# Up-projection blocks of a gated MLP: both 12-bit parts of the tokens in one 512-column product

## The chip, the cores and the metric

The kernel runs on one core of one Trainium2 chip. The metric is the device time of one execution in microseconds. The engines are TensorE (PE; its weight loads, which overlap the products, are listed as PEld), VectorE (DVE), ScalarE (ACT), GpSimd (POOL) and SyncE (SP, which here issues the DMAs).

## The reference, cut to what matters

Two decoder layers over 256 tokens of width 1024, in float32. A layer has a mixer (retention, attention and short convolution), an output projection with layer norm, and a gated MLP with layer norm. The change is in the MLP:

```
def conv_ffn(h, w_up, ffn_conv_w, w_down):
    u = h @ w_up
    a, b = u[..., :D_FF], u[..., D_FF:]
    a = causal_dwconv(a, ffn_conv_w)
    return (jax.nn.gelu(a.astype(F32), approximate=False) * b.astype(F32)).astype(h.dtype) @ w_down
```

D_FF is 2816, that is 22 feature tiles of 128; the contraction over D_MODEL = 1024 has 8 K tiles of 128; causal_dwconv has three taps.

## The kernel before, in words

Every float32 operand of the large products is held as two parts in the type float32r, a high part and the remainder (`split`, L80 to L82: an ACT copy makes the high part, a DVE subtraction the low one). A product of two such operands is three products: high by high, low by high, and high by low.

The weights come as units of 128 rows by 1024 columns in the order of the list `units` (L86 to L110). `prepare` (L120) loads a unit by DMA into one of five `raw` buffers and splits it into `whi` (L81, ACT) and `wlo` (L82, DVE), of which there are SLOTS = 6 each. `weights` (L143) asks for the units up to LOOKAHEAD = 5 beyond the one that is wanted now. So the cast of a unit waits until PE is done with the unit that had its buffer before.

The tokens, transposed, are the tiles `xh` and `xl` (128 partitions, 8 K tiles, 256 tokens). They are written at the start by `load_first` (L151) and afterwards by `turn` (L561), which transposes 128 tokens on PE and splits the result; both are allocated anew for each half of a layer (L555, L665).

In the MLP of a layer, feature tiles 0 and 1 are computed ahead with the tokens as the stationary operand (`first_up`, L584), tile 2 by halves (L626). Then a loop over f (L650) computes the up projection of tile f+1 (`up`, L621: two calls of `feature_block`, L297, one for a and one for b), takes the down-projection weights of tile f, and adds tile f's part to four PSUM banks (L658 to L660: `out_mm`, which calls `mm3`, L229, four times, so 12 products of 512 columns). The last tiles' down products are held back and done after the loop. A `feature_block` is 8 K tiles of three products of 256 columns (L302 to L304), summed in the left half of a PSUM bank (`acc`, four banks). `gated` (L606) turns a and b into h: z = a times tap 2 (L608, ACT), two more taps (L609 and L611, DVE), Gelu (L613, ACT), times b (L615, DVE), and the split into `hh` (L81, ACT) and `hl` (L82, DVE), which are the stationary operands of the down products.

The program is traced in this order; a planner of the framework then fixes the order in each engine's queue by its own estimate of times, and puts in the waits.

Of the kernel before, what the change touches and what calls it, by code (L numbers as in the profile page):

```python
# [11 lines left out]
F32R = mybir.dt.float32r  # L12
# [4 lines left out]
P = 128  # L17
D = 1024
T = 256
# [7 lines left out]
KD = D // P  # L27
# [17 lines left out]
FILL = (2, 1, 1, 2)  # L45
AT = ((7, 8), (7, 8), (6, 8), (20, 22))
WARM = 6
HALVES = (slice(0, HD), slice(HD, P))


@with_exitstack
def hybrid_decoder(ctx: ExitStack, tc: tile.TileContext, x, xT, wv, wf, wt, w_out, wg, w_up, w_down,
                   conv_w, ffn_w, ln1_g, ln1_b, ln2_g, ln2_b, rel_bias,
                   c_ident, c_rot, c_decay, c_bucket, out):
    nc = tc.nc
    cp = ctx.enter_context(tc.tile_pool(name="cp", bufs=1))
    wp = ctx.enter_context(tc.tile_pool(name="wp", bufs=1))
    xp = ctx.enter_context(tc.tile_pool(name="xp", bufs=1))
# [6 lines left out]
    def acc():  # L65
        return pa.tile([P, 512], F32, name="acc", tag="acc")

    def att():
        return pb.tile([P, 512], F32, name="att", tag="att")

    def big(dtype, name):
        return wp.tile([P, 1024], dtype, name=name, tag="big", bufs=2 * TAIL)
# [7 lines left out]
    def split(dst_hi, dst_lo, src):  # L80
        nc.scalar.copy(dst_hi, src)  # L81
        nc.vector.tensor_sub(dst_lo, src, dst_hi.bitcast(F32))  # L82
# [37 lines left out]
    def prepare(upto):  # L120
        while state["next"] < min(upto, len(units)):
            key, src, held = units[state["next"]]
            r = raw()
            if held:
                hi, lo = big(F32R, "hhi"), big(F32R, "hlo")
            else:
                hi = wp.tile([P, 1024], F32R, name="whi", tag="whi", bufs=SLOTS)
                lo = wp.tile([P, 1024], F32R, name="wlo", tag="wlo", bufs=SLOTS)
            if len(src.shape) == 2:
                nc.sync.dma_start(r, src)  # L130
                convert(key, hi, lo, r, 1024)
            elif state["next"] < KD:
                load_first(state["next"], r, src, hi, lo)
            else:
                k, c = src.shape[1:]
                nc.sync.dma_start(r[:, :k * c].rearrange("p (k c) -> p k c", k=k), src)
                convert(key, hi, lo, r, k * c)
            ready[key] = (hi, lo)
            state["next"] += 1
            if state["next"] >= 7 and spread:  # L140
                spread.pop(0)()

    def weights(*key, ahead=LOOKAHEAD):  # L143
        prepare(index[key] + 1 + ahead)
        return ready.pop(key)


    xh = xp.tile([P, KD, T], F32R, name="xh", tag="xh")
    xl = xp.tile([P, KD, T], F32R, name="xl", tag="xl")

    def load_first(k, r, src, hi, lo):  # L151

# [19 lines left out]
    def warm_up():  # L172
# [3 lines left out]
        ps = att()  # L176
        for i in range(WARM):
            nc.tensor.matmul(ps[:, :P], zero, zero, start=True, stop=True)
# [80 lines left out]
    def fetch_table(func, after):  # L259

        nc.scalar.activation(sp.tile([P, 1], F32, name="table", tag="table", bufs=1), after[:, :1], func)
# [11 lines left out]
    for k in range(KD):  # L273
        hi, lo = weights(0, "v", k)
        for g in range(NV):
            c = slice(g * VG, g * VG + VG)
# [7 lines left out]
    for l in range(DEPTH):  # L284
# [12 lines left out]
        def feature_block(*name):  # L297
            hi, lo = weights(l, *name)
            ps = acc()
            for k in range(KD):  # L300
                c = slice(k * P, k * P + P)
                nc.tensor.matmul(ps[:, :T], hi[:, c], xh[:, k, :], start=k == 0, stop=False)  # L302
                nc.tensor.matmul(ps[:, :T], hi[:, c], xl[:, k, :], start=False, stop=False)  # L303
                nc.tensor.matmul(ps[:, :T], lo[:, c], xh[:, k, :], start=False, stop=k == KD - 1)  # L304
            return ps
# [6 lines left out]
        class Pair:  # L312
# [9 lines left out]
            def scores(self, ps, c128, c256):  # L322

                for lhs, rhs, c, first, last in (
# [3 lines left out]
                        (self.narrow_hi, self.wide_lo, c256, False, True)):  # L328
                    for r, p in zip(HALVES, ps):
                        nc.tensor.matmul(p[:, c], lhs[r], rhs[r], start=first, stop=last)  # L330

        def buf256(name):
            return ap.tile([P, T], F32, name=name, tag="b256", bufs=3)

        moba = [Pair() for _ in range(3)]
        for i, m in enumerate(moba):
            p = feature_block(f"mq{i}")[:, :T]
# [4 lines left out]
        for i, m in enumerate(moba):  # L342
            p = feature_block(f"mk{i}")[:, :T]
# [113 lines left out]
        def moba_values(j):  # L457

            po = att()
            for t, s in ((0, slice(0, T)), (1, slice(T, 3 * P))):  # L460
                for h, r in zip((2 * j, 2 * j + 1), HALVES):
                    nc.tensor.matmul(po[r, t * P:T], mv[t][:, h * HD:h * HD + HD], prob[h][:, s],
# [60 lines left out]
        for t, p in enumerate(token_group("rg")):  # L523
            c, g = slice(t * HW, t * HW + HW), slice(t * NH, t * NH + NH)
            y, gt = yn[:, c], gate[:, c]
# [11 lines left out]
        ps = [[acc() for _ in range(2)] for _ in range(NT)]  # L537
# [5 lines left out]
        def late_mm(t):  # L543
            return [lambda h=h, n=n: out_mm(t, h, *late[n], False, n == len(late) - 1)
                    for h in range(2) for n in range(len(late))]

        for n, k in enumerate(WO_ORDER[:-TAIL]):
            hi, lo = weights(l, "wo", k)
# [3 lines left out]
        late = [weights(l, "wo", k) + (ch[:, k, :], cl[:, k, :]) for k in WO_ORDER[-TAIL:]]  # L552
        gw = [weights(l, "g", i, ahead=SLOTS - 1 - i) for i in range(4)]
        x1 = xp.tile([P, NT, D], F32, name="x1", tag="xtok", bufs=2)
        xh = xp.tile([P, KD, T], F32R, name="xh", tag="xh")  # L555
        xl = xp.tile([P, KD, T], F32R, name="xl", tag="xl")

        def norm(t, xin, g, b, xout):
            layer_norm(t, ps[t], xin, g, b, xout)
# [4 lines left out]
        def weave(steps, t, xout, at):  # L564

            for i, step in enumerate(steps):
                for h in range(2):
                    if at[h] == i:
                        turn(t, xout, h)
                step()  # L570
            for h in range(2):
                if at[h] >= len(steps):
                    turn(t, xout, h)
# [32 lines left out]
        def gated(f, a, b):  # L606
            z = sp.tile([P, T], F32, name="za", tag="f256", bufs=6)
            nc.scalar.mul(z, a, fw[:, l, f, 2:3])  # L608
            nc.vector.scalar_tensor_tensor(z[:, 1:], a[:, :T - 1], fw[:, l, f, 1:2], z[:, 1:],  # L609
                                           op0=ALU.mult, op1=ALU.add)  # L610
            nc.vector.scalar_tensor_tensor(z[:, 2:], a[:, :T - 2], fw[:, l, f, 0:1], z[:, 2:],  # L611
                                           op0=ALU.mult, op1=ALU.add)
            nc.scalar.activation(z, z, AF.Gelu)  # L613
            hf = sp.tile([P, T], F32, name="hf", tag="f256", bufs=6)
            nc.vector.tensor_mul(hf, z, b)  # L615
            hh = sp.tile([P, T], F32R, name="hh", tag="hh", bufs=LAST + 1)
            hl = sp.tile([P, T], F32R, name="hl", tag="hl", bufs=LAST + 1)
            split(hh, hl, hf)
            return hh, hl

        def up(f):  # L621
            a = feature_block("up", f, 0)[:, :T]
            return gated(f, a, feature_block("up", f, 1)[:, :T])

        a = []
# [6 lines left out]
        ps = [[att() for _ in range(2)] for _ in range(NT)]  # L632

        def value_group(vt, vw, g, t):

            bank = []

            def step(k):
                if k == 0:
                    bank.append(acc())  # L640
                hi, lo = vw[g][k // 4]
                c = slice(k % 4 * VG, k % 4 * VG + VG)
                mm3(bank[0][:, :VG], xh[:, k, tokens(t)], xl[:, k, tokens(t)], hi[:, c], lo[:, c],
                    k == 0, k == KD - 1)
                if k == KD - 1:
                    nc.scalar.copy(vt[t][:, g * VG:g * VG + VG], bank[0][:, :VG])
            return [lambda k=k: step(k) for k in range(KD)]
# [14 lines left out]
        if l + 1 < DEPTH:  # L662
            fetch_table(AF.Exp, late[-1][2].bitcast(F32))
            vw = [[weights(l + 1, "v", g, i, ahead=SLOTS - 1 - 2 * g - i) for i in range(2)] for g in range(NV)]
            xh = xp.tile([P, KD, T], F32R, name="xh", tag="xh")  # L665
            xl = xp.tile([P, KD, T], F32R, name="xl", tag="xl")
            for step in late_mm(0):
                step()
            norm(0, x1, g2, b2, x2)
            weave(late_mm(1), 0, x2, AT[1])  # L670
            norm(1, x1, g2, b2, x2)
            vt = [big(F32, "v") for _ in range(NT)]
            for t in range(NT):
                steps = []
                for g in range(NV):
                    steps += value_group(vt, vw, g, t)
                if t == 0:
                    weave(steps, 1, x2, AT[3])
                else:
                    for step in steps:  # L680
                        step()
        else:
            for t in range(NT):
                for step in late_mm(t):
                    step()
                layer_norm(t, ps[t], x1, g2, b2, x2, lambda s: nc.sync.dma_start(out[tokens(t), s], x2[:, t, s]))
# [72 lines left out]
```

## Time and profile before

| | us |
|---|---|
| median of 3 runs | 631.47 (631.27 to 631.86) |
| the profiled execution, its own time | 632.78 |
| span of the profiled execution | 631.0 |
| PE busy | 617.9 |
| DVE busy | 436.1 |
| ACT busy | 332.3 |

The span runs from the first to the last instruction of the profiled execution; its own time has some 1.8 us around it. A matmul's record overlaps the next one's, so its duration (283 ns for 256 columns) isn't what it costs; the distance between starts is. The granted TensorE clock is given as a share of full speed, 0.996 over the span. L302 is line 302 of the kernel before.

### The profile page before, as it was taken

What the parts mean: (1) busy time and instruction counts of PE and PEld (TensorE: products, weight loads), DVE (VectorE), ACT (ScalarE), POOL (GpSimd) and SP (SyncE); (2) the same over time, 40 slices, a digit from 0 to 9 for tenths busy, and PEclk for the clock granted to TensorE, in tenths of its full rate; (3) what the DMA queues carried; (4) which work ended last, traced back from release to release, by engine and by line L of the source; (5) the groups of instructions that cost most, each with busy time, mean ns of one, the idle gap of its engine ahead of it and who ended that gap; (6) DMA issues with size and microseconds to landing.
All of it is one profiled execution on the core that took longest, in us unless ns stands there. A gap on an engine that the chain in (4) does not pass through costs nothing.

```text
span 631.0 us, 11073 instructions
## 1 busy us (share of the span) xinstructions
PE 617.9 (98%) x4350; PEld 574.1 (91%) x4350; DVE 436.1 (69%) x774; ACT 332.3 (53%) x581; POOL 14.1 (2%) x14
## 2 busy tenths in 40 slices
PE   8999999999999999999999999999999999999994
PEld 7898899879999999999899999987999999999993
DVE  4468789877566565677766687888865665657746
ACT  4569936245544545466336795371745445455620
POOL 0000002000000000000000000101000000000001
PEclk9999999999999999999999999999999999999998
DMA  6996545745655555567427435572656565556401
GB/s 209 282 380 231 163 158 182 263 131 197 202 176 196 175 193 177 190 227 273 135 68 265 139 106 161 159 254 117 220 184 193 178 194 176 196 181 195 159 1 66
DMA packets 37163, 115.99 MB, mean 184 GB/s; under 512 B 4049, under 2 KB 9464, under 8 KB 37112
## 3 DMA queue, kind: packets, MB, share of 16 engines
q1 hardware_dynamic: 37112, 115.30, 55.3%
q8 instruction: 34, 0.56, 0.4%
q14 instruction: 17, 0.14, 0.1%
HBM read 114.22 MB, written 1.06 MB: 183 GB/s over the span
## 4 chain that ended last, share of the span: by engine, by line
PE 86%; DMA 5%; DVE 4%; ACT 1%; SPq 1%; issue 1%; POOL 0%; DVEq 0%; ACTq 0%; POOLq 0%
PE acc L304 13%; PE acc L303 13%; PE acc L302 13%; PE att L230 6%; PE att L231 6%; PE att L232 6%; PE acc L231 5%; PE acc L232 5%; PE acc L230 5%; PE acc L391 4%; PE acc L392 4%; PE acc L393 4%; DMA raw<-in_wf_dram 3%; DMA raw<-in_wv_dram 2%; PE att L330 1%
## 5 line engine op out<-in xcount | busy, mean ns | idle before, releaser
L82 DVE TENSOR_TENSOR wlo<-raw,whi 128x1024 fp32r<-128x1024 f32 (+3 forms) x207 | 229.5, 1115 | 138.2 <-ACT whi L81 137.6
L81 ACT CAST whi<-raw 128x1024 fp32r<-128x1024 f32 (+3 forms) x207 | 197.6, 962 | 197.1 <-PE acc L303 102.9
L304 PE MATMUL acc<-xh,wlo 128*128 128x256 f32 x720 | 203.7, 283 | 0.0
L303 PE MATMUL acc<-xl,whi 128*128 128x256 f32 x720 | 203.7, 283 | 0.0
L302 PE MATMUL acc<-xh,whi 128*128 128x256 f32 x720 | 203.6, 283 | 0.0
L302 PEld LDWEIGHTS acc<-xh,whi 128*128 128x128 f32 x720 | 138.1, 192 | 1.4
L303 PEld LDWEIGHTS acc<-xl,whi 128*128 128x128 f32 x720 | 138.1, 192 | 1.3
L304 PEld LDWEIGHTS acc<-xh,wlo 128*128 128x128 f32 x720 | 138.1, 192 | 0.2
L391 PE MATMUL acc<-xh,whi 128*128 128x256 f32 x208 | 61.3, 295 | 0.0
L392 PE MATMUL acc<-xl,whi 128*128 128x256 f32 x208 | 58.8, 283 | 0.0
L393 PE MATMUL acc<-xh,wlo 128*128 128x256 f32 x208 | 58.8, 283 | 0.0
L231 PE MATMUL att<-whi,hl 128*128 128x512 f32 x144 | 56.5, 392 | 0.0
L232 PE MATMUL att<-wlo,hh 128*128 128x512 f32 x144 | 56.0, 389 | 0.0
L230 PE MATMUL att<-whi,hh 128*128 128x512 f32 x144 | 55.7, 394 | 0.0
L230 PE MATMUL acc<-whi,xh 128*128 128x256 f32 (+2 forms) x144 | 47.1, 331 | 1.2 <-ACT whi L81 1.2
L231 PE MATMUL acc<-whi,xl 128*128 128x256 f32 (+2 forms) x144 | 46.3, 324 | 0.8 <-DVE xl L82 0.8
L232 PE MATMUL acc<-wlo,xh 128*128 128x256 f32 (+2 forms) x144 | 45.8, 323 | 0.1
L391 PEld LDWEIGHTS acc<-xh,whi 128*128 128x128 f32 x208 | 39.6, 190 | 2.6 <-issue 1.0
L392 PEld LDWEIGHTS acc<-xl,whi 128*128 128x128 f32 x208 | 39.6, 191 | 0.2
L393 PEld LDWEIGHTS acc<-xh,wlo 128*128 128x128 f32 x208 | 39.6, 191 | 0.1
L232 PEld LDWEIGHTS att<-wlo,hh 128*128 128x128 f32 x144 | 27.1, 188 | 5.8
L230 PEld LDWEIGHTS att<-whi,hh 128*128 128x128 f32 x144 | 27.0, 189 | 4.8
(136 smaller groups left out, 805.3 us busy)
## 6 DMA issues: line engine op xcount, KB each, us to landing
raw<-in_w_up_dram SPq DMA_DIRECT2D x80, 512.0 KB, 3.7
raw<-in_w_down_dram SPq DMA_DIRECT2D x44, 512.0 KB, 3.7
raw<-in_wf_dram SPq DMA_DIRECT2D x36, 512.0 KB, 4.4
raw<-in_w_out_dram SPq DMA_DIRECT2D x16, 512.0 KB, 4.2
raw<-in_wg_dram SPq DMA_DIRECT2D x8, 512.0 KB, 4.3
raw<-in_wt_dram SPq DMA_DIRECT2D x8, 384.0 KB, 3.1
raw<-in_wv_dram SPq DMA_DIRECT2D x6, 512.0 KB, 4.8
raw<-in_wv_dram SPq DMA_DIRECT2D x7, 384.0 KB, 5.6
```

Source lines behind the costliest of these rows:

```text
L81: nc.scalar.copy(dst_hi, src)
L82: nc.vector.tensor_sub(dst_lo, src, dst_hi.bitcast(F32))
L230: nc.tensor.matmul(ps, lhi, rhi, start=first, stop=False)
L231: nc.tensor.matmul(ps, llo, rhi, start=False, stop=False)
L232: nc.tensor.matmul(ps, lhi, rlo, start=False, stop=last)
L302: nc.tensor.matmul(ps[:, :T], hi[:, c], xh[:, k, :], start=k == 0, stop=False)
L303: nc.tensor.matmul(ps[:, :T], hi[:, c], xl[:, k, :], start=False, stop=False)
L304: nc.tensor.matmul(ps[:, :T], lo[:, c], xh[:, k, :], start=False, stop=k == KD - 1)
L330: nc.tensor.matmul(p[:, c], lhs[r], rhs[r], start=first, stop=last)
L391: nc.tensor.matmul(ps[:, :T], hi[:, c], xh[:, k, :], start=k == 0, stop=False)
L392: nc.tensor.matmul(ps[:, :T], hi[:, c], xl[:, k, :], start=False, stop=False)
L393: nc.tensor.matmul(ps[:, :T], lo[:, c], xh[:, k, :], start=False, stop=k == KD - 1)
```

## The change

The tiles `xh` and `xl` become the two halves of one tile `xx` (128 partitions, 8 K tiles, 2 parts, 256 tokens). For feature tiles 3 to 17 of both layers, `up` calls `wide_block`: per K tile one product of the high weight part with both token parts (512 columns, a whole PSUM bank) and one of the low weight part with the high token part (256 columns, added to the right half). Then an ACT copy takes the right half out of PSUM into a tile `feat` (three buffers, of a tag that the mixer uses too), and a DVE addition adds the left half to it. `gated` reads a and b from these tiles in place of PSUM. Feature tiles 0 to 2 and 18 to 21 stay as they were.

```diff
+WIDE = range(3, 18)
...
-    xh = xp.tile([P, KD, T], F32R, name="xh", tag="xh")
-    xl = xp.tile([P, KD, T], F32R, name="xl", tag="xl")
+    def parts():
+
+        x = xp.tile([P, KD, 2, T], F32R, name="xx", tag="xx")
+        return x, x[:, :, 0, :], x[:, :, 1, :]
+
+    xx, xh, xl = parts()
...
+        def wide_block(*name):
+
+
+            hi, lo = weights(l, *name)
+            ps = acc()
+            for k in range(KD):
+                c = slice(k * P, k * P + P)
+                nc.tensor.matmul(ps, hi[:, c], xx[:, k].rearrange("p s t -> p (s t)"), start=k == 0, stop=False)
+                nc.tensor.matmul(ps[:, T:], lo[:, c], xx[:, k, 0, :], start=False, stop=k == KD - 1)
+            y = buf256("feat")
+            nc.scalar.copy(y, ps[:, T:])
+            nc.vector.tensor_add(y, ps[:, :T], y)
+            return y
+
         def up(f):
+            if f in WIDE:
+                a = wide_block("up", f, 0)
+                return gated(f, a, wide_block("up", f, 1))
             a = feature_block("up", f, 0)[:, :T]
             return gated(f, a, feature_block("up", f, 1)[:, :T])
```

The two later allocations of `xh` and `xl` (L555, L665) become calls of `parts` in the same way.

## Rows read from the trace of the kernel before

**Rows 1.** The page: span, busy times, and the chain that ended last by engine.
```profile
span 631.0 us, 11073 instructions
...
PE 617.9 (98%) x4350; PEld 574.1 (91%) x4350; DVE 436.1 (69%) x774; ACT 332.3 (53%) x581; POOL 14.1 (2%) x14
...
PE 86%; DMA 5%; DVE 4%; ACT 1%; SPq 1%; issue 1%; POOL 0%; DVEq 0%; ACTq 0%; POOLq 0%
```

**Rows 2.** Windows: one loop turn, layer 0; the loop's stretch of layer 1.
```profile
core 0: us, PE busy (x) PEld busy (x) DVE busy (x) ACT busy (x) POOL busy (x), PEclk, DMA share, GB/s
157.00:165.50 8.50, 8.50 (x63) 8.01 (x62) 5.21 (x9) 4.14 (x6) 0.00 (x0) 1.00 0.68 227
464.00:583.00 119.00, 119.00 (x843) 112.13 (x842) 74.18 (x100) 58.95 (x85) 0.00 (x0) 1.00 0.58 189
```

**Rows 3.** Waits, 464 to 583 us, the whole answer: total us, times, longest.
```profile
DVE wlo L82 <- ACT whi L81: 44.3, 42, 1.4
ACT whi L81 <- PE acc L303: 42.2, 28, 1.6
ACT whi L81 <- PE att L231: 17.8, 14, 1.3
```

**Rows 4.** Groups by line and shape: busy us, mean ns, idle before.
```profile
L302 PE MATMUL acc<-xh,whi 128*128 128x256 f32 x720 | 203.6, 283 | 0.0
```

**Rows 5.** Timeline of PE, one loop turn of layer 0: start us, duration us.
```profile
200.07 0.40 PE L230 MATMUL att<-whi,hh 128*128 128x512 f32 x1
200.31 0.40 PE L231 MATMUL att<-whi,hl 128*128 128x512 f32 x1
200.54 0.39 PE L232 MATMUL att<-wlo,hh 128*128 128x512 f32 x1
...
202.59 0.39 PE L232 MATMUL att<-wlo,hh 128*128 128x512 f32 x1
202.82 0.28 PE L302 MATMUL acc<-xh,whi 128*128 128x256 f32 x1
202.93 0.28 PE L303 MATMUL acc<-xl,whi 128*128 128x256 f32 x1
...
208.57 0.40 PE L230 MATMUL att<-whi,hh 128*128 128x512 f32 x1
```

**Rows 6.** Timeline of PE, output projection of layer 0: first and last of 39 starts.
```profile
105.95 0.39 PE L232 MATMUL acc<-wlo,cath 128*128 128x512 f32 x1
...
114.79 0.39 PE L232 MATMUL acc<-wlo,cath 128*128 128x512 f32 x1
```

**Rows 7.** Groups by line and shape: a PSUM copy and a DVE operation on PSUM.
```profile
L615 DVE TENSOR_TENSOR hf<-za,acc 128x256 f32<-128x256 f32 x44 | 18.2, 413 | 2.5 <-PE acc L304 1.4 <-ACT za L613 1.1
...
L646 ACT COPY v<-acc 128x256 f32<-128x256 f32 x6 | 2.2, 370 | 5.5 <-PE acc L232 5.4
```

**Rows 8.** Timeline of all engines, layer 0, gating chain of one feature tile.
```profile
155.73 0.47 ACT L608 ACTIVATE za<-acc,fw 128x256 f32<-128x256 f32 x1
...
157.65 1.05 ACT L81 CAST whi<-raw 128x1024 fp32r<-128x1024 f32 x1 [1.46 <-PE acc L303]
...
160.29 1.05 ACT L81 CAST whi<-raw 128x1024 fp32r<-128x1024 f32 x1 [1.27 <-PE att L231]
...
162.52 0.42 DVE L82 TENSOR_TENSOR hl<-hf,hh 128x256 fp32r<-128x256 f32 x1
...
163.27 1.05 ACT L81 CAST whi<-raw 128x1024 fp32r<-128x1024 f32 x1 [1.63 <-PE acc L303]
...
166.07 0.40 PE L230 MATMUL att<-whi,hh 128*128 128x512 f32 x1
```

**Rows 9.** Timeline of all engines, layer 1 value projection with the last turn.
```profile
326.21 0.36 PE L230 MATMUL acc<-whi,xh 128*128 128x256 f32 x1
...
326.50 0.59 ACT L81 CAST xh<-att 128x512 fp32r<-128x512 f32 x1 [0.57 <-PE att L268]
```

**Rows 10.** Timeline of PE, loop start of layer 0.
```profile
150.09 0.28 PE L303 MATMUL acc<-xl,whi 128*128 128x256 f32 x1
150.27 1.19 PE L230 MATMUL att<-whi,hh 128*128 128x512 f32 x4
151.30 0.28 PE L304 MATMUL acc<-xh,wlo 128*128 128x256 f32 x1
```

More of the change, by code (lines that the diff above doesn't have):

```diff
@@ L554, in hybrid_decoder @@
         x1 = xp.tile([P, NT, D], F32, name="x1", tag="xtok", bufs=2)
-        xh = xp.tile([P, KD, T], F32R, name="xh", tag="xh")
-        xl = xp.tile([P, KD, T], F32R, name="xl", tag="xl")
+        xx, xh, xl = parts()
         def norm(t, xin, g, b, xout):
@@ L664, in hybrid_decoder @@
             vw = [[weights(l + 1, "v", g, i, ahead=SLOTS - 1 - 2 * g - i) for i in range(2)] for g in range(NV)]
-            xh = xp.tile([P, KD, T], F32R, name="xh", tag="xh")
-            xl = xp.tile([P, KD, T], F32R, name="xl", tag="xl")
+            xx, xh, xl = parts()
             for step in late_mm(0):
```

## The prediction, made before the change was run

> **What bounds the kernel now.** I read the page first. TensorE (PE) is busy 617.9 of 631.0 us, and the chain that ended last runs 86% over PE [rows 1]. A busy PE proves little by itself, since matmul records overlap, so I went on to the stage that the change touches: the loop over feature tiles f, once per layer. In its windows PE is busy all the time, at the full granted clock (1.00), while DVE has 5.21 and ACT 4.14 of 8.50 us and DMA stands at 0.58 to 0.68 [rows 2]. Then the waits of that stage: ACT's weight casts wait for PE to free a weight buffer, and DVE waits for ACT [rows 3]. PE is in no row of that answer, which has these three rows in all for 119 us. So PE sets the pace there, and what counts is the distance from one product's start to the next, not the 283 ns of a record [rows 4].
>
> The timeline of PE gives that distance [rows 5]. From 202.82 to 208.57 us stand two up blocks, 48 products of 256 columns: 5.75 us / 48 = 119.8 ns each. Ahead of them, from 200.07 to 202.82, stand the 12 products of 512 columns of one down-projection step. One turn of the loop is 8.50 us. In a long run of 512-column products, 39 starts from 105.95 to 114.79, the distance is 8.84 / 39 = 226.7 ns [rows 6]. So 256 more columns cost 226.7 - 119.8 = 106.9 ns, which is 2.4 columns per ns, and 119.8 - 106.9 = 12.9 ns come with each product and its weight load, whatever its width. **That 12.9 ns is what the change can take away**; the columns stay.
>
> **The change part by part.** Per K tile the three products (256 columns each) become one of 512 (high weight part times both token parts) and one of 256 (low part times high tokens), with two weight loads for three.
>
> Before, a K tile takes 3 x 119.8 = 359.4 ns. After, if each product keeps the price of its own long run, 226.7 + 119.8 = 346.5 ns: 12.9 ns less. There are 15 feature tiles x 2 blocks x 2 layers x 8 K tiles = 480 such K tiles: 480 x 12.9 ns = **6.2 us less on PE**. It lies wholly on the path, since PE waits for nothing there.
>
> No stretch before alternates the two widths, so I bound the price by the starts next to a change of width [rows 5]. Dear end: the first two 512-column products behind 256-column ones take 200.07 to 200.54, 235 ns each; 3 x 119.8 - 235 - 119.8 = 4.6 ns, x 480 = 2.2 us less. Cheap end: the first 256-column product behind 512-column ones takes 202.82 to 202.93, 110 ns; 359.4 - 226.7 - 110 = 22.7 ns, x 480 = 10.9 us less. Both are transients of one or a few products, and the long runs lie between them, so I take 12.9 ns and keep both ends.
>
> Added per block, 60 in all: an ACT copy of 128x256 out of PSUM (370 ns, by the copy of L646) and a DVE add of the same size (413 ns, by L615, which also reads a PSUM operand) [rows 7]. That makes 0.74 us of ACT and 0.83 us of DVE per turn: ACT 4.14 + 0.74 = 4.88, DVE 5.21 + 0.83 = 6.04, in a turn of 8.50 - 16 x 0.0129 = 8.29 us. Neither fills it. I cost them at nothing; PE's products hide them. Without that cover they would be 60 x 0.78 = 47 us.
>
> What waits behind them: on ACT the next weight cast stands behind the copy. That cast fills a buffer that PE needs some five units later (LOOKAHEAD = 5, a block of 2.88 us each), so 0.4 us doesn't reach PE. The path that has a deadline is the gating chain of the tile itself (L608 to the split of hf). In the turn shown, z starts at 155.73, the last step hl starts at 162.52 and takes 0.42, so it ends at 162.94, and the first product that reads hl follows the one at 166.07 by 0.23 us [rows 8]: slack 166.30 - 162.94 = 3.36 us. A copy and an add ahead of it make it 0.78 us later, and the turn is 0.21 us shorter: 2.4 us of slack remain. Cost nothing. The PSUM banks (four, two per turn) come free at the add, no later than before.
>
> The DMA issues stay as many and as large; a turn shorter by 2.4% lifts a DMA share of 0.58 to some 0.60 [rows 2], and nothing in that stage waits for a transfer [rows 3]. Nothing.
>
> The merged token tile (xh and xl as halves of one tile) changes no instruction's size. It could only cost if reads of one half were made to wait for writes of the other. The trace shows such tracking to be by element rather than by range: the product at 326.21 reads xh of the first 128 tokens and starts before the ACT cast at 326.50, queued earlier in the program, writes the same K tiles' other 128 tokens in between [rows 9]. Nothing, in load_first and in the turns alike.
>
> **Sum.** The profiled execution took 632.78 us (span 631.0): 632.78 - 6.2 = 626.6. The median of the runs is 1.3 us lower, 631.47, so **625.3 us**; the ends are 631.47 - 10.9 = 620.6 and 631.47 - 2.2 = 629.3.
>
> **The rivals.** (1) The 12.9 ns doesn't leave with the product. In an alternating stream every 512-column product could be paid as the one at 200.07 to 200.31 is, 0.24 us, as much as the two products that it replaces [rows 5]: saved 0, 631.5 us, no change. For it: every 512-column product would now stand right behind a 256-column one. Against: within the same down step the distance falls back to the long run's. Chance 0.07. [...]
>
> (2) Slower: the gating chain comes late. ACT and DVE work their queues in a fixed order, and casts that wait for PE stand in them at 157.65, 160.29 and 163.27 [rows 8]. If the later z, gelu or hh falls behind one cast more, the chain loses up to 163.27 - 160.29 = 2.98 us beside its own 0.78: 3.76 against 3.36 - 0.21 = 3.15, so PE waits 0.6 us in each of 30 turns: 631.47 - 6.2 + 18 = 643 us. It decides from the point where the chain loses a whole cast's turn; one queue place among short operations isn't enough. Against it: the order in the queues is planned and not the program's own, as the four down products at 150.27 in the midst of an up block show [rows 10], so a late chain can be planned around. Chance 0.09.
>
> (3) The wide product could be split in the build into two of 256 columns: 631.5 us, no change. The 512-column rows of the down step are single records [rows 5], so 0.02.
>
> **How the numbers follow.** Forecast 0.82, rivals 0.07, 0.09 and 0.02. About 0.2% (1.26 us) is what a measurement of this kernel can tell from no change. The forecast with both ends lies beyond that on the fast side: faster 0.82. No change: (1) and (3), 0.09. Slower: (2), 0.09. The range is the forecast's own, 620.6 to 629.3; it leaves the rivals out, 0.18 together.
>
> **What would show it.** Right: L302 to L304 keep 720 - 480 = 240 records each; the wide block's two lines have 480 each; a turn of the loop takes near 8.29 us; PE waits for nothing in the stage; ACT and DVE gain 60 operations each, some 22 and 25 us. In the PE timeline a 512- and a 256-column start together span 347 ns. Wrong: a pair at 355 to 360 ns (rival 1); PE or its weight loads waiting for hh or hl (rival 2); twice the wide records (rival 3); a stage outside the loop that changes by over a microsecond.

## The result and the profile after

The changed kernel takes 628.57 us (median of five runs, 628.15 to 629.26), the kernel before 631.86 us beside it (631.27 to 632.47): a ratio of 0.9946, 95% interval 0.9935 to 0.9958. It is faster, by 3.3 us where 6.2 were forecast. The profiled execution is the slowest of the five, 629.26 us; its page, to be read beside [rows 1], has the span, the busy times, and the chain by engine:

```profile
span 627.5 us, 10205 instructions
...
PE 614.0 (98%) x3870; PEld 547.3 (87%) x3870; DVE 456.5 (73%) x834; ACT 352.0 (56%) x641; POOL 14.1 (2%) x14
...
PE 88%; DVE 5%; DMA 3%; ACT 1%; issue 1%; SPq 1%; POOL 0%; DVEq 0%; ACTq 0%; POOLq 0%
```

PE has 4350 - 3870 = 480 products and 480 weight loads less, as counted. DVE gained 20.4 us and ACT 19.7 us for the 60 adds and 60 copies; their records below are 25.1 and 21.5 us, and overlap their neighbours in part. Line numbers have moved by some: the down products of L230 to L232 are now L235 to L237, the wide product is L632, the narrow one L633, the copy L635, the add L636. In the groups by line and shape (busy us, mean ns, idle before):

```profile
L632 PE MATMUL acc<-xx,whi 128*128 128x512 f32 x480 | 170.8, 398 | 0.0
...
L633 PE MATMUL acc<-xx,wlo 128*128 128x256 f32 x480 | 134.9, 281 | 0.0
...
L636 DVE TENSOR_TENSOR feat<-acc,feat 128x256 f32<-128x256 f32 x60 | 25.1, 418 | 0.0
L635 ACT COPY feat<-acc 128x256 f32<-128x256 f32 x60 | 21.5, 358 | 0.0
```

The waits of the loop's stretch in layer 1, 464 to 580 us, which answer to [rows 3], have these five rows and no more:

```profile
DVE wlo L83 <- ACT whi L82: 25.7, 28, 1.4
ACT whi L82 <- PE acc L632: 20.9, 14, 1.6
ACT za L612 <- DVE feat L636: 19.0, 14, 1.4
DVE za L613 <- ACT za L612: 7.5, 13, 0.6
ACT whi L82 <- PE att L236: 7.3, 14, 0.5
```

PE still waits for nothing there. The new step shows as a wait of ACT for DVE (z waits for the sum of the two halves), which costs nothing, since no wait of PE follows from it. So the missing 3 us are not in a wait. They are in the distances on PE. The timeline of PE in the changed kernel, with the two up blocks of one turn (16 pairs) from 200.57 to 206.21, and the starts of the down step of two turns, 13 turns apart:

```profile
164.28 0.40 PE L235 MATMUL att<-whi,hh 128*128 128x512 f32 x1
...
200.57 0.39 PE L632 MATMUL acc<-xx,whi 128*128 128x512 f32 x1
200.80 0.28 PE L633 MATMUL acc<-xx,wlo 128*128 128x256 f32 x1
200.91 0.40 PE L632 MATMUL acc<-xx,whi 128*128 128x512 f32 x1
201.14 0.28 PE L633 MATMUL acc<-xx,wlo 128*128 128x256 f32 x1
201.26 0.40 PE L632 MATMUL acc<-xx,whi 128*128 128x512 f32 x1
201.50 0.28 PE L633 MATMUL acc<-xx,wlo 128*128 128x256 f32 x1
201.62 0.40 PE L632 MATMUL acc<-xx,whi 128*128 128x512 f32 x1
...
206.21 0.40 PE L235 MATMUL att<-whi,hh 128*128 128x512 f32 x1
...
273.31 0.40 PE L235 MATMUL att<-whi,hh 128*128 128x512 f32 x1
```

A pair takes 5.64 us / 16 = 352.5 ns, not 346.5. The first pair behind the down products takes 200.57 to 200.91, 0.34 us; the next ones 0.35 and 0.36: the wide product stays as dear as the first ones behind narrow products were in the kernel before [rows 5]. A turn is 109.03 us / 13 = 8.387 us against 110.50 / 13 = 8.500 before (166.07 in [rows 8] to 276.57): 0.113 us less where 0.206 were forecast.

```profile
276.57 0.40 PE L230 MATMUL att<-whi,hh 128*128 128x512 f32 x1
```

Thirty turns make 3.4 us, about the measured difference.

### The profile page after: what moved, and what is told of

It is laid out like the page before. It is cut to its first block, busy times and chain, and to the rows that moved or that the text cites. A ratio compares the mean times of both kernels' runs of the same rounds, so it can differ in the third digit from the quotient of the medians.

```text
span 627.5 us, 10205 instructions
## 1 busy us (share of the span) xinstructions
PE 614.0 (98%) x3870; PEld 547.3 (87%) x3870; DVE 456.5 (73%) x834; ACT 352.0 (56%) x641; POOL 14.1 (2%) x14
## 4 chain that ended last, share of the span: by engine, by line
PE 88%; DVE 5%; DMA 3%; ACT 1%; issue 1%; SPq 1%; POOL 0%; DVEq 0%; ACTq 0%; POOLq 0%
PE acc L632 18%; PE acc L633 9%; PE att L235 6%; PE att L236 6%; PE att L237 6%; PE acc L308 5%; PE acc L309 5%; PE acc L307 5%; PE acc L396 4%; PE acc L236 4%; PE acc L237 4%; PE acc L235 4%; PE acc L397 4%; PE acc L398 4%; PE att L335 1%; DMA raw<-in_w_up_dram 1%
## 5 line engine op out<-in xcount | busy, mean ns | idle before, releaser
L632 PE MATMUL acc<-xx,whi 128*128 128x512 f32 x480 | 170.8, 398 | 0.0
L633 PE MATMUL acc<-xx,wlo 128*128 128x256 f32 x480 | 134.9, 281 | 0.0
L632 PEld LDWEIGHTS acc<-xx,whi 128*128 128x128 f32 x480 | 90.2, 188 | 21.9
L633 PEld LDWEIGHTS acc<-xx,wlo 128*128 128x128 f32 x480 | 90.8, 189 | 1.3
L308 PE MATMUL acc<-xx,whi 128*128 128x256 f32 x240 | 68.0, 283 | 0.0
L309 PE MATMUL acc<-xx,wlo 128*128 128x256 f32 x240 | 68.0, 283 | 0.0
L307 PE MATMUL acc<-xx,whi 128*128 128x256 f32 x240 | 68.0, 283 | 0.0
L396 PE MATMUL acc<-xx,whi 128*128 128x256 f32 x208 | 61.4, 295 | 0.0
L397 PE MATMUL acc<-xx,whi 128*128 128x256 f32 x208 | 58.9, 283 | 0.0
L398 PE MATMUL acc<-xx,wlo 128*128 128x256 f32 x208 | 58.8, 283 | 0.0
L237 PE MATMUL att<-wlo,hh 128*128 128x512 f32 x144 | 56.1, 390 | 0.0
L235 PE MATMUL att<-whi,hh 128*128 128x512 f32 x144 | 55.7, 394 | 0.0
L235 PE MATMUL acc<-whi,xx 128*128 128x256 f32 (+2 forms) x144 | 46.9, 330 | 1.6 <-ACT whi L82 1.6
L236 PE MATMUL acc<-whi,xx 128*128 128x256 f32 (+2 forms) x144 | 46.1, 323 | 0.8 <-DVE xx L83 0.8
L307 PEld LDWEIGHTS acc<-xx,whi 128*128 128x128 f32 x240 | 46.1, 192 | 0.1
L308 PEld LDWEIGHTS acc<-xx,whi 128*128 128x128 f32 x240 | 46.1, 192 | 0.1
L309 PEld LDWEIGHTS acc<-xx,wlo 128*128 128x128 f32 x240 | 46.1, 192 | 0.0
L237 PE MATMUL acc<-wlo,xx 128*128 128x256 f32 (+2 forms) x144 | 45.6, 321 | 0.1
L396 PEld LDWEIGHTS acc<-xx,whi 128*128 128x128 f32 x208 | 39.6, 190 | 2.6 <-issue 1.0
```

Of the source, the lines that this page charges most:

```text
L235: nc.tensor.matmul(ps, lhi, rhi, start=first, stop=False)
L236: nc.tensor.matmul(ps, llo, rhi, start=False, stop=False)
L237: nc.tensor.matmul(ps, lhi, rlo, start=False, stop=last)
L632: nc.tensor.matmul(ps, hi[:, c], xx[:, k].rearrange("p s t -> p (s t)"), start=k == 0, stop=False)
L633: nc.tensor.matmul(ps[:, T:], lo[:, c], xx[:, k, 0, :], start=False, stop=k == KD - 1)
```

## The experiments

In each of them the edit is against the changed kernel. Theories: A, a change of the product's width costs time on PE by itself; B, a narrow product is dear because it adds to PSUM columns just written; C, the added copy and add take PE's time; D, a narrow product is too short to cover the next weight load.

**Grouped: all wide products of a block, then all narrow ones.**

```diff
-            for k in range(KD):
-                c = slice(k * P, k * P + P)
-                nc.tensor.matmul(ps, hi[:, c], xx[:, k].rearrange("p s t -> p (s t)"), start=k == 0, stop=False)
-                nc.tensor.matmul(ps[:, T:], lo[:, c], xx[:, k, 0, :], start=False, stop=k == KD - 1)
+            for k0 in range(0, KD, 8):
+                for k in range(k0, k0 + 8):
+                    c = slice(k * P, k * P + P)
+                    nc.tensor.matmul(ps, hi[:, c], xx[:, k].rearrange("p s t -> p (s t)"), start=k == 0, stop=False)
+                for k in range(k0, k0 + 8):
+                    c = slice(k * P, k * P + P)
+                    nc.tensor.matmul(ps[:, T:], lo[:, c], xx[:, k, 0, :], start=False, stop=k == KD - 1)
```

> The changed kernel has a mean of 352.5 ns for a 512- and a 256-column product together, where the long runs of each width give 226.7 + 119.8 = 346.5 ns. Here a block does its 8 wide products first and its 8 narrow ones after them: one change of width each way per block in place of eight. Theory A (each change of width costs some ns, whatever the operands): a block takes 8 x 226.7 + 8 x 119.8 + about 18 ns (what one change each way cost in the kernel before) = 2.79 us against 8 x 352.5 = 2.82 us, so 60 x 0.03 = 1.8 us less than the changed kernel, about 626.8 us, and the wide products stand 227 ns apart. Theory B (the narrow product is dear because it adds to PSUM columns that the wide one has just written): here only the first narrow product of a block does so, about the same time; the run doesn't tell A from B. Theory C (the added ACT copy and DVE add disturb PE, so the distances stay long in any order): no change, 628.6 us.

Measured: 626.05 us (four runs, 625.54 to 626.70) against 631.46 beside it, ratio 0.9915 (0.990 to 0.993), clear of the changed kernel's interval. The timeline of PE (products of one line in a row are one row, x8), and the ends of 13 turns:

```profile
164.29 0.40 PE L235 MATMUL att<-whi,hh 128*128 128x512 f32 x1
...
208.57 1.98 PE L633 MATMUL acc<-xx,whi 128*128 128x512 f32 x8
210.38 1.11 PE L636 MATMUL acc<-xx,wlo 128*128 128x256 f32 x8
211.33 2.00 PE L633 MATMUL acc<-xx,whi 128*128 128x512 f32 x8
...
272.27 0.40 PE L235 MATMUL att<-whi,hh 128*128 128x512 f32 x1
```

Eight wide products right behind the down products take 208.57 to 210.38, 226 ns each, and eight narrow ones 210.38 to 211.33, 119 ns: the long runs' prices. A turn is 107.98 / 13 = 8.306 us, and 30 x (8.387 - 8.306) = 2.4 us; the medians differ by 2.5. Same columns, same loads, same copies and adds: only the order differs. C falls here for the distances. A had said 1.8 us, so it had the sign and the size, not more.

**Left half: the narrow product adds to the other half of the bank.**

```diff
-                nc.tensor.matmul(ps[:, T:], lo[:, c], xx[:, k, 0, :], start=False, stop=k == KD - 1)
+                nc.tensor.matmul(ps[:, :T], lo[:, c], xx[:, k, 0, :], start=False, stop=k == KD - 1)
```

> The narrow product adds to the left half of the bank in place of the right one, so to columns that the wide product wrote 512 and not 256 columns earlier; the sum of both halves is the same. Theory A (width changes cost): nothing changes, 352.5 ns per pair, 628.6 us. Theory B (columns just written): the pair falls to 346.5 ns, 480 x 6 ns = 2.9 us less, 625.7 us. Theory C: no change.

Measured: 628.17 us (627.40 to 629.23), ratio 0.9950 (0.9933 to 0.9966), the changed kernel's. In PE's timeline the pairs are the same:

```profile
200.89 0.39 PE L632 MATMUL acc<-xx,whi 128*128 128x512 f32 x1
201.12 0.28 PE L633 MATMUL acc<-xx,wlo 128*128 128x256 f32 x1
201.23 0.40 PE L632 MATMUL acc<-xx,whi 128*128 128x512 f32 x1
201.47 0.28 PE L633 MATMUL acc<-xx,wlo 128*128 128x256 f32 x1
201.58 0.40 PE L632 MATMUL acc<-xx,whi 128*128 128x512 f32 x1
```

0.34 and 0.35 us per pair, as before the edit. B falls for the half of the bank: which of the two the narrow product adds to makes no difference. That it adds to the same bank at all, this run leaves open; the next one answers it.

**Widths: the second product made wider.**

```diff
+            w = (384, 512)[l]
...
+                both = xx[:, k].rearrange("p s t -> p (s t)")
...
-                nc.tensor.matmul(ps[:, T:], lo[:, c], xx[:, k, 0, :], start=False, stop=k == KD - 1)
+                nc.tensor.matmul(ps[:, 512 - w:], lo[:, c], both[:, 512 - w:], start=False, stop=k == KD - 1)
```

> The second product of each K tile is made wider: 384 columns in layer 0 (it adds the low part of the weights times the low part of the tokens, and leaves out the low part times the first 128 tokens' high part), 512 columns in layer 1 (all of both token parts, one term more than needed). Long runs have 226.7 ns for 512 and 173.3 ns for 384 columns. Theory A: the 512 + 384 pair is dearer than 400 ns by some 3 to 8 ns, the 512 + 512 pair takes 453.4 ns with nothing on top. Theory D (only a 256-column product is too short to cover the next weight load, so the excess ends above it): 400 ns and 453.4 ns, nothing on top of either. Theory B: something on top of both, since both write columns just written.

The whole time (663.77 us, one run) says nothing, since it has more columns; the distances do. The ends of 12 turns in layer 0, and in layer 1 the last 16 up products of a turn up to its down step, of PE's timeline:

```profile
165.57 0.40 PE L235 MATMUL att<-whi,hh 128*128 128x512 f32 x1
...
276.29 0.40 PE L235 MATMUL att<-whi,hh 128*128 128x512 f32 x1
```
```profile
471.24 0.39 PE L634 MATMUL acc<-xx,whi 128*128 128x512 f32 x1
...
474.87 0.39 PE L235 MATMUL att<-whi,hh 128*128 128x512 f32 x1
```

Layer 1: 16 products from 471.24 to 474.87, 226.9 ns each, nothing on top, though the weights change with each of them and both products of a pair write the same 512 columns: B falls altogether. Layer 0: a turn of 110.72 / 12 = 9.227 us, where 28 wide products and 16 of 384 columns at the long runs' prices make 28 x 226.7 + 16 x 173.3 = 9.120; 0.107 us on top, 6.7 ns per pair. The 173.3 ns are from a long run of such products in the kernel before, 42 from 95.64 to 102.92:

```profile
95.64 0.33 PE L230 MATMUL acc<-whi,xh 128*128 128x384 f32 x1
...
102.92 0.33 PE L230 MATMUL acc<-whi,xh 128*128 128x384 f32 x1
```

The excess doesn't end above 256 columns, so D falls as the expectation puts it; equal widths have none, as A says. But a weight load's record in this run is 188 ns long, more than the 120.0 and 173.3 ns of products of 256 and 384 columns and less than the 226.7 ns of a wide one:

```profile
L635 PEld LDWEIGHTS acc<-xx,wlo 128*128 128x128 f32 x480 | 90.1, 188 | 10.0
```

So the run doesn't exclude that a load longer than the product beside it plays a part at a change of width. By itself it costs nothing: the long runs of 256, 384 and 512 columns (120.0, 173.3 and 226.7 ns) lie on one line, with 13.3 ns on top of 2.4 columns per ns at each width. Two different widths that are both above or both below the load's length would tell these two readings apart; that was not run.

**Added work: three products again, with all the rest of the change kept.**

```diff
-                nc.tensor.matmul(ps, hi[:, c], xx[:, k].rearrange("p s t -> p (s t)"), start=k == 0, stop=False)
+                nc.tensor.matmul(ps[:, :T], hi[:, c], xx[:, k, 0, :], start=k == 0, stop=False)
+                nc.tensor.matmul(ps[:, T:], hi[:, c], xx[:, k, 1, :], start=False, stop=False)
```

> The blocks of tiles 3 to 17 keep the merged token tile, the ACT copy and the DVE add, but take three products of 256 columns per K tile again (one into the left half, two into the right). It prices all that the change added. If PE covers it: distances of 120 ns and the time of the kernel before, 631.5 us, no change within 0.2%. If the added work takes PE's time (theory C): slower than the kernel before by what the change fell short, about 3 us, 634.4 us.

Measured: 631.55 us (11 runs) against 631.94 (15 runs), ratio 0.9995 (0.9986 to 1.0004): no change. PE's timeline has the turn of the kernel before to the nanosecond, 110.50 / 13 = 8.500 us:

```profile
164.15 0.40 PE L235 MATMUL att<-whi,hh 128*128 128x512 f32 x1
...
274.65 0.40 PE L235 MATMUL att<-whi,hh 128*128 128x512 f32 x1
```

The copies, the adds and the merged token tile together cost nothing that can be measured, and C falls altogether.

**How the price goes with the length of a run: paired, fours, crossed.** Paired takes two wide products, then two narrow ones; fours the same with four. Crossed takes the wide products of both blocks of a feature tile, then the narrow ones of both.

The edit of paired, in which the loop of the changed kernel is replaced; fours has 4 for 2:

```diff
+            for k0 in range(0, KD, 2):
+                for k in range(k0, k0 + 2):
+                    c = slice(k * P, k * P + P)
+                    nc.tensor.matmul(ps, hi[:, c], xx[:, k].rearrange("p s t -> p (s t)"), start=k == 0, stop=False)
+                for k in range(k0, k0 + 2):
+                    c = slice(k * P, k * P + P)
+                    nc.tensor.matmul(ps[:, T:], lo[:, c], xx[:, k, 0, :], start=False, stop=k == KD - 1)
```

> Two wide products, then two narrow ones, four times per block: half of the width changes of the changed kernel, four times those of the grouped one. An alternating pair has 6.0 ns on top of the long-run distances per change there and back; a change there and back between runs of eight or more has 18 ns. If each change costs the same whatever the run (3 ns), a block has 4 x 6 = 24 ns on top, 2.796 us; if the cost grows with the run behind it, four times some 8 to 12 ns, 2.80 to 2.82 us. Theory A asks for a value between 2.79 us (grouped) and 2.82 us (alternating) in either case; about 627 us.

> Both blocks of a tile together: wide products of a, wide products of b, narrow ones of a, narrow ones of b. With the down products, which are 512 columns too, one change of width there and back per turn in place of the grouped kernel's two. Theory A: 30 turns x 18 ns = 0.5 us less than the grouped kernel (626.05 us), 625.5 us. Against it: the low parts' buffers come free later and the copy of a comes later by 8 x 0.227 = 1.8 us; if that eats the slack of the gating chain (2.4 us by the sum before), PE waits for hl and it is slower than the grouped kernel.

> Four wide products, then four narrow ones, twice per block. By the long-run distances (12 + 16 products at 226.7 ns, 16 at 120.0) a turn of the loop is 8.267 us. On top of that the changed kernel has 0.120 us in 16 changes there and back (7.5 ns each), the paired one 0.026 us in 8 (3.3 ns each), the grouped one 0.040 us in 2 (20 ns each). If the price of a change there and back is a matter of the run's length, it lies between 3.3 and 20 ns here, 4 of them per turn: a turn of 8.280 to 8.347 us. If only the count of changes mattered, runs of four would lie between the paired and the grouped kernel, 8.293 to 8.307 us.

PE's timeline, the ends of 13 turns of paired, of fours and of crossed:

```profile
165.05 0.40 PE L235 MATMUL att<-whi,hh 128*128 128x512 f32 x1
...
272.87 0.40 PE L235 MATMUL att<-whi,hh 128*128 128x512 f32 x1
```
```profile
164.59 0.40 PE L235 MATMUL att<-whi,hh 128*128 128x512 f32 x1
...
273.19 0.40 PE L235 MATMUL att<-whi,hh 128*128 128x512 f32 x1
```
```profile
166.96 0.40 PE L235 MATMUL att<-whi,hh 128*128 128x512 f32 x1
...
274.68 0.40 PE L235 MATMUL att<-whi,hh 128*128 128x512 f32 x1
```

Turns, with what they have on top of the long runs' prices (28 x 226.7 + 16 x 120.0 ns = 8.267 us; 12 x 226.7 + 48 x 120.0 = 8.480 us before). The 120.0 ns are (208.57 - 202.93) / 47 of [rows 5]; the prediction's 119.8 has the first, cheap start in it.

| order | changes there and back per turn | turn, us | on top, ns | per change, ns |
|---|---|---|---|---|
| kernel before | 1 | 8.500 | 20 | 20 |
| changed kernel: 1 wide, 1 narrow | 16 | 8.387 | 120 | 7.5 |
| paired | 8 | 8.294 | 27 | 3.4 |
| fours | 4 | 8.354 | 87 | 22 |
| grouped: 8 and 8 | 2 | 8.306 | 39 | 20 |
| crossed: 28 wide, 16 narrow | 1 | 8.286 | 19 | 19 |

Between runs of four or more a change there and back costs some 20 ns whatever their length. Runs of one and two pay less per change. For pairs the rows say where it goes. Timeline of PE of paired, with two products in a row of the answer:

```profile
201.64 0.63 PE L633 MATMUL acc<-xx,whi 128*128 128x512 f32 x2
202.11 0.39 PE L636 MATMUL acc<-xx,wlo 128*128 128x256 f32 x2
...
206.29 0.39 PE L636 MATMUL acc<-xx,wlo 128*128 128x256 f32 x2
206.52 0.40 PE L235 MATMUL att<-whi,hh 128*128 128x512 f32 x1
```

Over the seven changes from 201.64 to 206.52, two wide products take 467 ns on average where the long run has 453, and two narrow ones 230 ns where it has 240. The dear starts and the cheap ones nearly cancel. I had expected neither price: fours lies above the range given for it, since I took the price to rise evenly with the run, and paired beats grouped.

In time: paired 626.04 us and fours 628.01, in a single run each, crossed 626.03 (six runs, but 624.23 to 628.96). Paired was run again with timing:

> The paired order again, now timed. Its turn of 8.293 us against 8.387 of the changed kernel gives 30 x 0.094 = 2.8 us less than the changed kernel's 628.6 us: 625.8 us. Against the grouped order (8.307 us) it is 30 x 0.014 = 0.4 us less. Whoever holds that the distances on PE are not what sets the time expects no difference from the changed kernel.

Measured: 626.32 us (six runs, 624.95 to 628.43), ratio 0.9907 (0.9891 to 0.9923). It is faster than the changed kernel by about what its turn says (2.8 expected, 2.3 measured); 0.4 us between paired and grouped is too little for runs that spread over 3.5 us.

Crossed has the shortest turn; the 30 x 0.02 = 0.6 us that it should win over grouped is too little for runs that spread over 4.7 us. In its trace of 275 to 300 us, past the up blocks of the wide tiles, PE waits for hl:

```profile
DVE hlo L83 <- ACT hhi L82: 3.6, 2, 1.9
...
PE att L236 <- DVE hl L83: 0.4, 1, 0.4
```

The copy of a comes later in this order, as the expectation said. But in this execution a down weight also landed late, and DVE waits 1.9 us for its cast in the midst of the chain that makes hl; which of the two made PE wait isn't shown.

**Grouped, up to feature tile 21.** Grouped's edit, and with it this one:

```diff
-WIDE = range(3, 18)
+WIDE = range(3, NF)
```

> The grouped order, and the wide blocks reach up to feature tile 21 in place of 17: 16 blocks more. Theory A: each saves 2.876 - 2.79 = 0.085 us, 1.4 us in all, 624.7 us against 626.05 for the grouped kernel. Against it: in the last tiles no down products stand between the up blocks, so DVE, busy 15.8 of the 21.0 us from 285 to 306 us in the kernel before, gets some 16 x 0.41 / 2 = 3.3 us more per layer; if that makes a weight part or hl late, PE waits and the 1.4 us are lost or turn into a loss.

Measured: 626.13 us (625.56 to 626.85), ratio 0.9907 (0.9894 to 0.9921): no gain over grouped. In layer 1 the gain came: from the loop's last down step (576.78) to the down products at the stage's end (601.85) PE takes 25.07 us, in grouped 25.78 (576.21 to 601.99). The waits from 275 to 315 us show that layer 0 lost its share:

```profile
ACT za L617 <- DVE za L615: 5.6, 5, 1.9
...
PE att L235 <- ACT hh L82: 0.8, 1, 0.8
```

ACT waits for the taps on DVE, and the down products at the stage's end wait for hh. That is rival (2), a late gating chain, in the stretch where the expectation had found DVE busy for 15.8 of 21.0 us.

## Why the prediction was right in its direction and too large

- **The bound, right.** PE sets the pace of the loop; each ns on its distances counts once. From the first down product of a layer's loop to the last turn's the changed kernel takes 137.25 us in layer 0 (144.55 to 281.80) and 128.74 in layer 1 (451.20 to 579.94), the kernel before 138.92 (146.15 to 285.07) and 130.42 (453.05 to 583.47): 1.67 and 1.68 us less, together the whole measured difference.
- **Added work at nothing, right.** The run with only the added work takes the time of the kernel before.
- **The merged tile, right**, by the same run.
- **Gating chain, right.** In the changed kernel's timeline hl ends at 160.84 + 0.42 = 161.26 us, and the first product that reads it follows the one at 164.28 by 0.23: a slack of 3.25 us, where 3.36 stood before and I had left 2.4. The two weight casts that stand in the chain on ACT, ahead of Gelu and of hh, wait for PE not at all and 0.50 us, where they waited 1.46 and 1.27 us before [rows 8], so the copy and the add found their time:

```profile
156.51 1.05 ACT L82 CAST whi<-raw 128x1024 fp32r<-128x1024 f32 x1
...
158.61 1.05 ACT L82 CAST whi<-raw 128x1024 fp32r<-128x1024 f32 x1 [0.50 <-PE att L236]
...
160.84 0.42 DVE L83 TENSOR_TENSOR hl<-hf,hh 128x256 fp32r<-128x256 f32 x1
```

- **The price of a pair, wrong in size.** The step that failed is "if each product keeps the price of its own long run, 226.7 + 119.8 = 346.5 ns", taken over the dear end because both ends were "transients of one or a few products". In an alternating stream no product has a long run behind it, so the transient is the steady state: 352.5 ns, so that 480 x (359.4 - 352.5) = 3.3 us went in place of 6.2. The order that avoids nearly all of it (paired) has a turn 0.206 us below the kernel before, which is the forecast. So the term of 12.9 ns per product was right (13.3 with 120.0 for a narrow one), and a second term, the change of width, was missing from the sum; the bounds held it. The dear bound was taken from two starts, where the dear starts behind a change are five (below).
- **Rival (1)** named the right place and had the price too high: of the 12.9 ns a little under half is lost in the changes, not all of it.
- **The signs.** A pair at 352.5 ns lies between the 347 of the forecast and the 355 to 360 of rival (1). One sign of being wrong did show: outside the loops two stretches differ by over a microsecond between the two profiled executions. The start of layer 0's loop comes 1.60 us earlier in the changed kernel, and the stretch between the loops is 1.42 us longer (281.80 to 451.20 and 285.07 to 453.05). Paired and paired_timed are one and the same kernel, and their two profiled executions differ there by as much: 1.49 us (145.45 and 146.94) and 0.95 us (167.97 and 168.92). So neither is put down to the change.
- **The Trainium skill**, "TensorE: Matmul & The Clock Gate", section "Back-to-back issue gap", gives columns / 2.4 plus 2.5 ns as the gap of an isolated product, and says that it counts too little at small widths and too much at large ones. As an estimate from it, 256 columns would stand 109.2 ns apart and 512 columns 215.8. At 256 columns the trace agrees that this is too little, with 120.0 ns; at 512 it doesn't agree that it is too much, with 226.7.

What stays open is why a change of width costs. The runs exclude the place in PSUM and the work of ACT and DVE, and a weight load longer than its product as a cause by itself. They don't tell what in PE is upset, nor whether the load plays a part at a change. For pairs the rows show how the price comes out small; for single products they leave it open.

Of the 1.42 us between the loops the waits show the most: at 429.50 and 431.42 us PE waits 0.47 and 0.56 us for the layer norm, behind an up weight that landed late. The profiles of left half and grouped don't have these waits.

## What to carry to other kernels

Where PE is the bound, a product and its weight load have a fixed price beside their columns (here 12.9 ns), so joining two narrow products with the same stationary operand saves one of two such prices. But read the price in the order in which the products will stand: mixing widths one by one gave back nearly half of the gain, and two or eight of one width in a row got most of it back with no more than a changed loop, 626.3 and 626.1 us for 628.6 (four in a row less of it, by the turn). And a transient in a trace, a few products long, becomes the steady state of a stream that changes at every step.

## What the runs showed of the hardware that I had not expected

In long runs, distances of products that each bring new weights are 120.0, 173.3 and 226.7 ns for 256, 384 and 512 columns, which is 2.4 columns per ns plus 13.3 ns. A change of width there and back costs some 20 ns between runs of four or more, 7.5 ns when the widths alternate and 3.4 ns in pairs; behind a change to 512 columns the first five products are dear, not two. In the kernel before they go from 200.07 [rows 5] to this sixth one:

```profile
201.23 0.39 PE L232 MATMUL att<-wlo,hh 128*128 128x512 f32 x1
```

That is 232 ns each, 27 ns in all above the long run, and the seven after them, to 202.82, take 227 each. Behind a change to 256 columns the first product is cheap (0.11 us, in [rows 5] and at 200.80 above). A run cut short after two wide products pays for two dear starts alone.
